# Spreading per-token factors over 64 partitions by DMAs through DRAM in a two-layer encoder kernel

## The chip, the cores and the metric

The kernel runs on one NeuronCore of a Trainium2 chip. The metric is device time in microseconds (us) of one launch. Its program drives five instruction streams that synchronise by semaphores: TensorE (PE, matmuls and transposes, results in PSUM), VectorE (DVE), ScalarE (ACT), GpSimd (POOL) and SyncE (SP), which here does nothing but start DMAs. Each stream runs in order: an instruction that waits holds up everything behind it on its stream.

## The reference

Two layers (`DEPTH` = 2) over 512 tokens of width 1024, all in float32. The part that matters is the first half of a layer, two attention mixers that share one input projection:

```python
proj = einsum('bsd,de->bse', x, w_in)            # q, k, v of both mixers and the gate logits
oa = banded_attention(qa, ka, va, 128, a_sink)   # 8 heads; per token and head: o / denom
for g, (window, dil) in enumerate(((128, 1), (512, 4), (2048, 16))):
    o[g], lse[g] = dilated_attention(qb[g], kb[g], vb[g], window, dil)   # 4 heads each
wts = softmax(stack(lse), axis=0)                # per token and head, over the three groups
ob = einsum('gbsh,gbshd->bshd', wts, stack(o))
h = (ga * (oa @ w_branch_a) + gb * (ob @ w_branch_b)) @ w_out
x = layer_norm(alpha * x + h)                    # then a squared-ReLU MLP and a second layer norm
```

So there are two sorts of factors that belong to one token and one head: `1/denom` of mixer A, and the three group weights (already divided by the softmax sums) of mixer B. Each multiplies the 64 channels of its head's output.

## The kernel before

**Layout.** Activations lie transposed: channels on the 128 partitions, the 512 tokens along the free dimension. Every matrix product is done as three matmuls of float32r halves (`mm3`, lines 279 to 281: high by high, low by high, high by low). A weight set of 128 x 1024 is fetched by SP (`wst`, L248, three buffers), then split by `split` into a rounded high part on ACT (`whi`, L227) and the rest on DVE (`wlo`, L228); `weights(key)` asks for the set two ahead of the one in use.

**Attention.** `unit_a(i)` (four of them) handles two heads of mixer A, `unit_b(sp, g)` (six) two heads of one dilated group. A unit computes scores into the two PSUM banks tagged `s` (`sa`, `sb`, L438), adds the mask and takes the row maximum on DVE (`masked`, L431), takes the exponential on ACT (`exped`, L427, which also sums the rows: the softmax denominators), turns the probabilities by PE transposes into a bank tagged `pt` (`probs_T`, L416) and multiplies them with the values into `f` (128 channels of two heads x 512 tokens). `mix_b(sp)` then makes the weights of the three groups for head pair `sp` (L664 to L699): a tile `e`, in which each partition is a token of one of four blocks and the 24 columns are group, head and block.

**The factors.** In `den` and `e` the tokens lie on partitions; `f` has them along the free dimension. So a factor has to be turned, and repeated over the 64 channels of its head. Before, `widened` (L455) copies the 8 factors of a partition to 512 columns on ACT, and `token_scaled` turns them with four PE transposes into a `pt` bank `rs` (L461) and multiplies `f` by it on DVE (L462). This is done 10 times in a layer: 4 in `unit_a`, 3 in each of the two `mix_b`. In `mix_b` the three scaled groups are then added on POOL (L708) and DVE (L709) and split into `OB[sp]` (`obh`, `obl`).

**What sets the order.** The PE's order in the attention is written out by generators: `fc`, a small forecast of the engines' times, decides when a step of a unit is `able`; in between the projections of the next units and gates (`filler`: `qb`, `kb`, `vb`, `g`, and `ya`, the products of `w_branch_a`) are put. Two units are live at once. The order of the other engines' instructions, SP's DMAs among them, is set by the compiler's scheduler. After the attention, `ya` and gate projections follow, and then `yb`, the first product that reads `OB` (L1099).

Of the kernel before, what the change touches and what calls it, by code (L numbers as in the profile page):

```python
# [10 lines left out]
F32 = mybir.dt.float32  # L11
# [9 lines left out]
P = 128  # L21
S = 512
# [15 lines left out]
HOP = 0.35  # L38
# [162 lines left out]
def build(nc, tc, plan, down, xT, xN, pT, wst, vec, rows, sink, cst, out):  # L201
# [3 lines left out]
    with ctx:  # L205
# [4 lines left out]
        def bank(tag, name):  # L210
            return pp.tile([P, 512], F32, tag=tag, name=name, bufs={"mm": 3, "s": 2, "pt": 2, "o": 1}[tag])


        ident = cp.tile([P, P], F32, name="ident")
# [11 lines left out]
        def split(hi, lo, src):  # L226
            nc.scalar.copy(hi, src)  # L227
            nc.vector.tensor_tensor(lo, src, hi.bitcast(F32), ALU.subtract)  # L228
# [119 lines left out]
        def attention_block(l, av, rp, vt, OA, OB, begun):  # L348
# [81 lines left out]
            def masked(dst, ps, mask, mx):  # L430
                nc.vector.tensor_tensor_reduce(dst, ps, mask, 1.0, NEG, ALU.add, ALU.max, mx)  # L431
                return fc.on("dve", 0.07 + mask.shape[-1] / 960, fc.t + HOP)
# [12 lines left out]
            def join(f, o, r):  # L445
                a, b = slice(r * 64, r * 64 + 64), slice(64 - r * 64, P - r * 64)
                nc.scalar.copy(f[a, :], o[b, :])
                nc.vector.tensor_tensor(f[a, :], o[a, :], f[a, :], ALU.add)
                t = fc.on("dve", 0.6, fc.on("act", 0.48, fc.t + HOP) + HOP) + HOP
                fc.give("o", t)  # L450
                return t

            def widened(c, name, after):
                wide = av.tile([P, 4, 2, 64], F32, tag="wide", name="wide" + name, bufs=1)
                nc.scalar.copy(wide, c.rearrange("p r (j u) -> p j r u", u=1).to_broadcast([P, 4, 2, 64]))  # L455
                return wide, fc.on("act", 0.52, after) + HOP

            def token_scaled(f, wide, name, after):
                R = bank("pt", "rs" + name)
                for j in range(4):  # L460
                    nc.tensor.transpose(R[:, j * P:(j + 1) * P], wide[:, j].rearrange("p r d -> p (r d)"), ident)  # L461
                nc.vector.tensor_tensor(f, f, R, ALU.mult)  # L462
                t = fc.on("dve", 0.6, max(fc.pe(0.43) + HOP, after)) + HOP
                fc.take("pt", t)
                return t


            WIN = [(max(0, P * (j - 1)), min(S, P * (j + 2))) for j in range(4)]
# [2 lines left out]
            def unit_a(i):  # L471
                q, k = held["qa", i], held["ka"]
                nm_ = f"a{l}_{i}"
# [4 lines left out]
                den = av.tile([P, 2, 4], F32, tag="den", name="den" + nm_, bufs=2)  # L478
                ns = nsink.rearrange("p (r i) -> p r i", r=2)[:, :, i]
                ap, ex = {}, {}  # L480
                for j in range(4):
# [6 lines left out]
                    for r in range(2):  # L488
                        ap[r, j] = pr[r][:, POS[j]:POS[j] + w]
                        t = masked(ap[r, j], ss[r][:, :w], cc["ma"][:, mo:mo + w], mx[:, r, j:j + 1])  # L490
                    fc.take("s", t + HOP)
                    nc.vector.scalar_tensor_tensor(nm[:, :, j], mx[:, :, j], -0.125, ns, ALU.mult, ALU.min)
                    t = fc.on("dve", 0.08, t + 0.13) + HOP
# [4 lines left out]
                nc.scalar.activation(se, se, AF.Exp)  # L498
                nc.vector.tensor_tensor(den, den, se, ALU.add)
                nc.vector.reciprocal(den, den)  # L500
                wide, t_wide = widened(den, nm_, ex[1, 3] + 0.6)
                yield lambda: "va" in held
                v, t_v = held["va"]
                f = av.tile([P, S], F32, tag="f", name="f" + nm_, bufs=1)
# [18 lines left out]
                for n, (r, kbs) in enumerate(groups):  # L523
# [7 lines left out]
                    c = 0  # L531
# [6 lines left out]
                    if n % 3 == 2:  # L538
                        t_f = join(f, o, r)
# [3 lines left out]
                held["P"] -= 2  # L543
                if i == 3:
                    held["vv"] -= 1
                yield lambda: fc.open("pt") and fc.t >= t_wide
                t_f = token_scaled(f, wide, nm_, t_f)
                split(OA[i][0], OA[i][1], f)
                forecast_split(S, t_f)

# [113 lines left out]
            def mix_b(sp, cn, cs):  # L664
                nm_ = f"{l}_{sp}"
                fs = [held["og", sp, g] for g in range(3)]
                t = max(x[2] for x in fs)
# [15 lines left out]
                t = fc.on("dve", 0.1, fc.pe(0.17) + HOP) + HOP  # L683
# [3 lines left out]
                e = av.tile([P, 3, 8], F32, tag="e", name="e" + nm_, bufs=1)  # L687
# [12 lines left out]
                t += 2.6  # L700
                for g in range(3):
                    f, t_f, _ = fs[g]
                    wide, t = widened(e[:, g].rearrange("p (s b) -> p s b", s=2), f"{nm_}_{g}", t)
                    yield lambda: fc.t >= t and fc.open("pt")
                    token_scaled(f, wide, f"{nm_}_{g}", t_f)
                    t = fc.t
                f = fs[0][0]
                nc.gpsimd.tensor_tensor(f, f, fs[1][0], ALU.add)  # L708
                nc.vector.tensor_tensor(f, f, fs[2][0], ALU.add)  # L709
# [7 lines left out]
            fc = Forecast()  # L717
# [79 lines left out]
            for i in range(4):  # L797
                waiting["a", i] = (slots(2, "ka", ("qa", i)), lambda i=i: unit_a(i))
# [240 lines left out]
        def pool(name, side="left"):  # L1039
            c = ExitStack()  # L1040
            return c.enter_context(tc.tile_pool(name=name, bufs=1, side=side, reuse_waits="tile")), c.close

        dp = ctx.enter_context(tc.tile_pool(name="dp", bufs=1, space=bass.MemoryType.DRAM))
# [14 lines left out]
        for l in range(DEPTH):  # L1058
# [13 lines left out]
            av, av_close = pool(f"av{l}")  # L1072
# [19 lines left out]
            for u in range(4):  # L1092
                gs = [gate(l, 1, t, vt, rp) for t in (2 * u, 2 * u + 1)]
                w = weights((l, ("bb", u)))
                for n, g in enumerate(gs):
                    t = 2 * u + n
# [268 lines left out]
```

## Time and profile before

| | |
|---|---|
| median of 3 runs | 1545.58 us (1545.32 to 1548.82) |
| profiled execution | 1545.51 us, its span 1543.7 us |
| mean granted TensorE clock | 0.996 |
| VectorE / ScalarE / GpSimd busy | 1089.2 us / 717.4 us / 205.4 us |
| DMA | 162.19 MB, mean 105 GB/s |

The span is what the profiler shows of the execution; 1.8 us lie around it. The attention of the two layers lies from about 28 to 259 us and from 797 to about 1028 us of the span; the rest is the branch and output projections, the gated embedding and the MLP. Which engine limits is read from the busy shares together with the chain of work that ended last: a high busy share of PE says that the PE's own work sets the time, and that a wait counts when the PE stands in it.

### The profile page before, as it was taken

How to read it: one execution, taken by the hardware profiler on the slowest of the kernel's cores; microseconds unless marked ns; L12 is line 12 of the kernel's file. 1: busy time of each engine (PE TensorE's matmuls, PEld its weight loads, DVE VectorE, ACT ScalarE, POOL GpSimd, SP SyncE). 2: the span in 40 equal slices, each digit the busy share in tenths (PEclk: the TensorE clock that was granted, in tenths of full speed). 3: DMA queues.
4: the chain of work that ended last, by engine and by line, in shares of the span. 5: the costliest groups of instructions: out<-in, count | busy, mean ns of one | idle time of the engine just before them, and what ended most of it. 6: DMA issues, size and time to landing. Idle time of an engine off the chain costs nothing.

```text
span 1543.7 us, 19566 instructions
## 1 busy us (share of the span) xinstructions
PE 1516.1 (98%) x7438; PEld 1244.0 (81%) x7438; DVE 1089.2 (71%) x1803; ACT 717.4 (46%) x1192; POOL 205.4 (13%) x161
## 2 busy tenths in 40 slices
PE   9999999999999999999999999999999999999996
PEld 7778788888888888888887778888888888888885
DVE  6778675467568767696877786744575776767868
ACT  4566554344334443434546665542442443444343
POOL 1011110020011120202010101111100211111022
PEclk9999999999999999999999999999999999999998
DMA  6211224244612415142342121254446233241403
GB/s 219 69 55 55 69 69 170 84 131 158 199 65 83 146 45 162 43 149 70 96 149 69 55 68 56 80 164 146 136 136 211 68 99 120 70 135 55 150 1 96
DMA packets 46461, 162.19 MB, mean 105 GB/s; under 512 B 5664, under 2 KB 6048, under 8 KB 46368
## 3 DMA queue, kind: packets, MB, share of 16 engines
q1 hardware_dynamic: 43200, 151.74, 29.3%
q0 software_dynamic: 2448, 8.91, 3.0%
q8 instruction: 58, 0.95, 0.2%
q10 hardware_dynamic: 720, 0.30, 0.1%
q14 instruction: 35, 0.29, 0.1%
HBM read 155.16 MB, written 4.19 MB: 103 GB/s over the span
## 4 chain that ended last, share of the span: by engine, by line
PE 87%; DVE 8%; ACT 2%; issue 1%; DMA 1%; ACTq 0%; SPq 0%; DVEq 0%
PE dn L1017 16%; PE ps_up L280 8%; PE ps_up L279 8%; PE ps_up L281 8%; PE pg L287 2%; PE wo L285 2%; PE wo L287 2%; PE wo L286 2%; PE pg L286 2%; PE pg L285 2%; DVE wlo L228 2%; PE sa L438 1%; PE pta L416 1%; PE ya L279 1%; PE ya L281 1%
## 5 line engine op out<-in xcount | busy, mean ns | idle before, releaser
L228 DVE TENSOR_TENSOR wlo<-wst,whi 128x1024 fp32r<-128x1024 f32 (+1 forms) x172 | 220.7, 1286 | 150.9 <-ACT whi L227 144.3
L227 ACT CAST whi<-wst 128x1024 fp32r<-128x1024 f32 (+1 forms) x172 | 175.7, 1022 | 299.5 <-PE ps_up L280 115.5
L279 PE MATMUL ps_up<-xhi,whi 128*128 128x512 f32 x512 | 199.2, 389 | 0.0
L280 PE MATMUL ps_up<-xlo,whi 128*128 128x512 f32 x512 | 199.2, 389 | 0.0
L281 PE MATMUL ps_up<-xhi,wlo 128*128 128x512 f32 x512 | 199.2, 389 | 0.0
L990 POOL TENSOR_TENSOR hr<-r 128x512 f32<-128x512 f32 x64 | 102.2, 1597 | 551.4 <-ACT r L982 530.9
L279 PEld LDWEIGHTS ps_up<-xhi,whi 128*128 128x128 f32 x512 | 96.1, 188 | 20.0
L281 PEld LDWEIGHTS ps_up<-xhi,wlo 128*128 128x128 f32 x512 | 96.1, 188 | 20.0
L280 PEld LDWEIGHTS ps_up<-xlo,whi 128*128 128x128 f32 x512 | 96.1, 188 | 19.8
L227 ACT CAST whi<-raw 128x1024 fp32r<-128x1024 f32 x56 | 58.0, 1053 | 97.0 <-PE ps_up L280 64.1
L227 ACT CAST dhi<-raw 128x1024 fp32r<-128x1024 f32 x56 | 58.7, 1051 | 82.2 <-PE dn L1017 59.8
L1036 DVE TENSOR_TENSOR y<-y,dn 128x512 f32<-128x512 f32 x96 | 65.2, 681 | 38.5 <-PE dn L1017 38.5
L970 DVE TENSOR_TENSOR raw<-raw,raw 128x1024 f32<-128x1024 f32 x64 | 86.4, 1349 | 0.2
L228 DVE TENSOR_TENSOR wlo<-raw,whi 128x1024 fp32r<-128x1024 f32 x56 | 68.1, 1219 | 14.1 <-ACT whi L227 14.1
L228 DVE TENSOR_TENSOR dlo<-raw,dhi 128x1024 fp32r<-128x1024 f32 x56 | 69.2, 1239 | 5.5 <-ACT dhi L227 5.5
L1017 PE MATMUL dn<-whi,smh 128*128 128x512 f32 x128 | 50.1, 394 | 0.7 <-DVE y L1036 0.7
L1017 PE MATMUL dn<-wlo,smh 128*128 128x512 f32 x128 | 50.6, 395 | 0.2
L287 PE MATMUL pg<-bhi,xlo 128*128 128x512 f32 x128 | 49.9, 390 | 0.6 <-DVE xlo L914 0.6
L1017 PE MATMUL dn<-whi,sml 128*128 128x512 f32 x128 | 49.9, 390 | 0.0
L285 PE MATMUL pg<-bhi,xhi 128*128 128x512 f32 x128 | 49.9, 390 | 0.0
L1017 PE MATMUL dn<-dhi,smh 128*128 128x512 f32 x128 | 49.9, 390 | 0.0
L1017 PE MATMUL dn<-dlo,smh 128*128 128x512 f32 x128 | 49.8, 389 | 0.0
(846 smaller groups left out, 3889.0 us busy)
## 6 DMA issues: line engine op xcount, KB each, us to landing
wst<-wst SPq DMA_DIRECT2D x187, 512.0 KB, 3.5
raw<-wst SPq DMA_DIRECT2D x64, 512.0 KB, 4.2
y<-rows POOLq DMA_DIRECT2D x14, 512.0 KB, 7.6
row<-rows SPq DMA_DIRECT2D x7, 512.0 KB, 9.8
wst<-wst SPq DMA_DIRECT2D x9, 256.0 KB, 2.7
xs<-xT SPq DMA_DIRECT2D x8, 256.0 KB, 5.7
y<-xN SPq DMA_DIRECT2D x4, 512.0 KB, 6.9
kept<-y SPq DMA_DIRECT2D x4, 512.0 KB, 2.9
```

Source lines behind the costliest of these rows:

```text
L227: nc.scalar.copy(hi, src)
L228: nc.vector.tensor_tensor(lo, src, hi.bitcast(F32), ALU.subtract)
L279: nc.tensor.matmul(ps, w[0][:, s], x[0], start=start, stop=False, skip_group_check=part)
L280: nc.tensor.matmul(ps, w[0][:, s], x[1], start=False, stop=False, skip_group_check=part)
L281: nc.tensor.matmul(ps, w[1][:, s], x[0], start=False, stop=stop, skip_group_check=part)
L285: nc.tensor.matmul(ps, x[0], w[0][:, c], start=start, stop=False)
L286: nc.tensor.matmul(ps, x[0], w[1][:, c], start=False, stop=False)
L287: nc.tensor.matmul(ps, x[1], w[0][:, c], start=False, stop=stop)
L970: nc.vector.tensor_tensor(to, to, other, ALU.add)
L990: nc.gpsimd.tensor_tensor(h.rearrange("p s t -> p (s t)"), r, r, ALU.mult)
L1017: nc.tensor.matmul(ps[s], a[:, k, tok], w[b][:, cols], start=first and not (k or m), stop=k == 3 and m == 2, skip_group_check=True)
L1036: return nc.vector.tensor_tensor(to, to, ps, ALU.subtract if n in (2, 4, 5) else ALU.add)
```

## The change

`widened` and `token_scaled` lose the copy and the transposes. A new function `spread_out` writes the 8 factors of each of 128 partitions into a DRAM tile `line` of 2 x 512 (head by token; each of the 1024 values is 4 bytes with no neighbour from the same partition), and then reads each head's row of 512 back onto 64 partitions of the tile `wide`. All three DMAs are started by SP. `line` has six buffers, `wide` one. The multiplication takes `wide` from SBUF instead of `rs` from PSUM. `dp` is the pool of DRAM tiles, which was there before.

```diff
-            def widened(c, name, after):
-                wide = av.tile([P, 4, 2, 64], F32, tag="wide", name="wide" + name, bufs=1)
-                nc.scalar.copy(wide, c.rearrange("p r (j u) -> p j r u", u=1).to_broadcast([P, 4, 2, 64]))
-                return wide, fc.on("act", 0.52, after) + HOP
-
-            def token_scaled(f, wide, name, after):
-                R = bank("pt", "rs" + name)
-                for j in range(4):
-                    nc.tensor.transpose(R[:, j * P:(j + 1) * P], wide[:, j].rearrange("p r d -> p (r d)"), ident)
+            def spread_out(c, name, after):
+
+                line = dp.tile([2, S], F32, tag="line", name="line" + name, bufs=6)
+                nc.sync.dma_start(line.rearrange("r (j p) -> p r j", j=4), c)
+                R = av.tile([P, S], F32, tag="wide", name="wide" + name, bufs=1)
+                for r in range(2):
+                    nc.sync.dma_start(R[r * 64:r * 64 + 64, :], line[r].partition_broadcast(64))
+                return R, after + 5.0
+
+            def token_scaled(f, R, after):
                 nc.vector.tensor_tensor(f, f, R, ALU.mult)
-                t = fc.on("dve", 0.6, max(fc.pe(0.43) + HOP, after)) + HOP
-                fc.take("pt", t)
-                return t
+                return fc.on("dve", 0.6, after) + HOP
...
-                wide, t_wide = widened(den, nm_, ex[1, 3] + 0.6)
+                R, t_R = spread_out(den, nm_, ex[1, 3] + 0.6)
...
-                yield lambda: fc.open("pt") and fc.t >= t_wide
-                t_f = token_scaled(f, wide, nm_, t_f)
+                t_f = token_scaled(f, R, max(t_f, t_R))
...
-                    wide, t = widened(e[:, g].rearrange("p (s b) -> p s b", s=2), f"{nm_}_{g}", t)
-                    yield lambda: fc.t >= t and fc.open("pt")
-                    token_scaled(f, wide, f"{nm_}_{g}", t_f)
-                    t = fc.t
+                    R, t_R = spread_out(e[:, g].rearrange("p (s b) -> p s b", s=2), f"{nm_}_{g}", t)
+                    token_scaled(f, R, max(t_f, t_R))
```

In the changed kernel the DMA to DRAM is L456, the DMAs that read it back are L459, and the multiplication is L463. Three places of the new order follow; layer 1 has the same order as layer 0.

SP, layer 0, at the weights of the first head pair (`mix_b(0)`); the names are the factors' tiles (`line_0_g`, `wide_0_g` of group g) and the weight sets `wst`. Before, only weight fetches stand here.

```order
L456 DMA line_0_0_1875<-e_0_1860 128x8x1 [waits DMAHW5_49,DVE_49,Activation_49]
L456 DMA line_0_1_1881<-e_0_1860 128x8x1 [waits DVE_49]
L456 DMA line_0_2_1887<-e_0_1860 128x8x1 [waits DVE_49]
L459 DMA wide_0_0_1877<-line_0_0_1875 64x512 [waits DMAHW5_49]
L459 DMA wide_0_0_1877<-line_0_0_1875 64x512
L248 DMA wst_2125<-wst 128x1024 [waits DMAHW2_49,DVE_49]
L459 DMA wide_0_1_1883<-line_0_1_1881 64x512 [waits DMAHW3_49,DMAHW1_49,DMAHW6_49,DMAHW0_49,DVE_49]
L459 DMA wide_0_1_1883<-line_0_1_1881 64x512 [waits DMAHW4_49]
L248 DMA wst_2187<-wst 128x1024 [waits DVE_49]
L459 DMA wide_0_2_1889<-line_0_2_1887 64x512 [waits DMAHW4_49,DMAHW7_49,DMAHW3_49,DVE_49]
```

All three `line` DMAs are started first, then the two halves of `wide_0_0`, which wait until its `line` has landed. `wide_0_1` waits on DVE, since the single buffer is free only after the multiplication of group 0, and `wide_0_2` after that of group 1.

DVE, layer 0, the same place, before the change (`ql_kb`: low part of the keys of the next unit; `pb` with `sb`: masking of that unit's scores; `cn`: its row maxima; `ogb`: the groups' outputs, multiplied in place):

```order
L462 TENSOR_TENSOR ogb_0_0_1362<-ogb_0_0_1362,rs_0_0_1935 128x512 [waits PE_49]
L228 TENSOR_TENSOR ql_kb_0_1913<-t_kb_0_1907,qh_kb_0_1912 128x512 [waits Activation_49]
L462 TENSOR_TENSOR ogb_0_1_1509<-ogb_0_1_1509,rs_0_1_1949 128x512 [waits PE_49]
L228 TENSOR_TENSOR wlo_2010<-wst_2007,whi_2009 128x1024 [waits DMAHW7_49,PE_49,Activation_49]
L431 ISA pb_1_0_0_1964,mxb_1_0_1963<-sb_1_0_0_0_1970,ct_157 128x192 [waits PE_49]
...
L462 TENSOR_TENSOR ogb_0_2_1751<-ogb_0_2_1751,rs_0_2_1993 128x512 [waits PE_49]
L584 TENSOR_SCALAR cn_1_328<-mxb_1_0_1963 128x2x2 [waits DVE_49]
```

And now, where the multiplications wait for DMAs:

```order
L228 TENSOR_TENSOR ql_kb_0_1925<-t_kb_0_1919,qh_kb_0_1924 128x512 [waits Activation_49]
L463 TENSOR_TENSOR ogb_0_0_1332<-ogb_0_0_1332,wide_0_0_1877 128x512 [waits DMAHW1_49,DMAHW0_49]
L228 TENSOR_TENSOR wlo_1966<-wst_1963,whi_1965 128x1024 [waits DMAHW3_49,PE_49,Activation_49]
L431 ISA pb_1_0_0_1974,mxb_1_0_1973<-sb_1_0_0_0_1980,ct_157 128x192 [waits PE_49]
...
L228 TENSOR_TENSOR vvvb_1_0_2008<-vtvb_1_0_2003,vvvb_1_0_2008 128x8x64 [waits Activation_49]
L463 TENSOR_TENSOR ogb_0_1_1504<-ogb_0_1_1504,wide_0_1_1883 128x512 [waits DMAHW4_49,DMAHW3_49]
L582 TENSOR_SCALAR cn_1_328<-mxb_1_0_1973 128x2x2 [waits DVE_49]
...
L463 TENSOR_TENSOR ogb_0_2_1728<-ogb_0_2_1728,wide_0_2_1889 128x512 [waits DMAHW7_49,DMAHW6_49]
L582 TENSOR_SCALAR cn_1_328<-mxb_1_0_1973 128x2x2 [waits DVE_49]
L373 STREAM_SHUFFLE sw_qb_1_2056<-ps_('qb', 1, 1)_1969 128x512 [waits PE_49]
```

The multiplication of group 0 now stands ahead of the masking of the next unit's first scores, the one of group 1 ahead of its first row maxima (the first `cn`), and the one of group 2 ahead of the second `cn`, on which the unit's remaining exponentials wait.

DVE, layer 0, at the second head pair (`mix_b(1)`), now (`gate` with `ya`: the first branch's products, taken out of PSUM; `wlo`: weight sets that PE needs one after the other):

```order
L463 TENSOR_TENSOR ogb_1_0_2049<-ogb_1_0_2049,wide_1_0_2607 128x512 [waits DMAHW4_49,DMAHW3_49]
L781 SCALAR_TENSOR_TENSOR gate_0_3_1756<-gate_0_3_1756,ya_1_1_2686 128x512 [waits PE_49]
L228 TENSOR_TENSOR wlo_2703<-wst_2700,whi_2702 128x1024 [waits DMAHW6_49,Activation_49]
L463 TENSOR_TENSOR ogb_1_1_2262<-ogb_1_1_2262,wide_1_1_2613 128x512 [waits DMAHW7_49,DMAHW6_49]
L463 TENSOR_TENSOR ogb_1_2_2478<-ogb_1_2_2478,wide_1_2_2619 128x512 [waits DMAHW2_49,DMAHW1_49]
L228 TENSOR_TENSOR wlo_2736<-wst_2733,whi_2735 128x1024 [waits PE_49,Activation_49]
L705 TENSOR_TENSOR ogb_1_0_2049<-ogb_1_0_2049,ogb_1_2_2478 128x512 [waits DVE_49,Pool_49]
```

The multiplications of groups 1 and 2 stand directly behind each other, though the second needs a reload of `wide` that starts after the first. The weight set `wlo_2736` stands behind both.

## The prediction

> **What bounds the kernel now.** I read first the page's busy shares, then its chain of work that ended last.
>
> ```profile
> PE 1516.1 (98%) x7438; PEld 1244.0 (81%) x7438; DVE 1089.2 (71%) x1803; ACT 717.4 (46%) x1192; POOL 205.4 (13%) x161
> PE 87%; DVE 8%; ACT 2%; issue 1%; DMA 1%; ACTq 0%; SPq 0%; DVEq 0%
> ```
>
> PE is never far from busy, and 87% of the chain is its own work. So PE time that goes is gained, unless a new wait brings PE to a stand; work that leaves ACT (46% busy) gains nothing by itself. The second share of the chain is DVE, and it lies largely in the attention, where the changed lines are. What matters is therefore how long PE stands when DVE or SP wait for the new DMAs.
>
> **What is removed.** The tile view of `rs` and `wide` counts it (durations are min/median/max in ns):
>
> ```profile
> L461 PE MATMUL rs<-ident,wide x48: 270/272/329, 180.1 to 1024.0; 128*128 128x128 f32 x48
> L461 PE MATMUL rsa<-ident,widea x32: 270/272/273, 70.7 to 905.5; 128*128 128x128 f32 x32
> L455 ACT COPY wide<-e x12: 616/618/620, 179.4 to 1022.7; 128x512 f32<-128x512 f32 x12
> L455 ACT COPY widea<-dena x8: 607/618/620, 57.2 to 886.4; 128x512 f32<-128x512 f32 x8
> L462 DVE TENSOR_TENSOR fa<-fa,rsa x8: 679/684/690, 75.4 to 909.3; 128x512 f32<-128x512 f32 x8
> ```
>
> 80 transposes are 20 groups of four. Durations of matmuls overlap, so a group's price is read from starts, in the timeline of PE (start, length, in us):
>
> ```profile
> 252.48 0.39 PE L281 MATMUL ya<-oah,wlo 128*128 128x512 f32 x1
> 252.71 0.60 PE L461 MATMUL rs<-ident,wide 128*128 128x128 f32 x4
> 253.06 0.48 PE L279 MATMUL ya<-oah,whi 128*128 128x512 f32 x1
> 253.38 0.39 PE L280 MATMUL ya<-oal,whi 128*128 128x512 f32 x1
> ...
> 253.61 0.40 PE L281 MATMUL ya<-oah,wlo 128*128 128x512 f32 x1
> ```
>
> A matmul of 512 columns starts 0.23 us after the one before (253.38 to 253.61). From 252.48 to 253.38 passed 0.90 where two such steps would take 0.46: the group costs **0.44 us**. The first group of each `mix_b` costs more, since PE also waits for the copy on ACT:
>
> ```profile
> 179.42 0.39 PE L281 MATMUL ps_('vb', 1, 0)_1922<-xhi,wlo 128*128 128x512 f32 x1
> ...
> 180.10 0.65 PE L461 MATMUL rs<-ident,wide 128*128 128x128 f32 x4 [0.29 <-ACT wide L455]
> ...
> 180.82 0.40 PE L280 MATMUL ps_('vb', 1, 0)_1922<-xlo,whi 128*128 128x512 f32 x1
> ...
> 249.99 0.39 PE L281 MATMUL ya<-oah,wlo 128*128 128x512 f32 x1
> ...
> 251.55 0.39 PE L280 MATMUL ya<-oal,whi 128*128 128x512 f32 x1
> ```
>
> 1.40 - 0.46 = 0.94 and 1.56 - 0.46 = 1.10. A layer has eight plain groups and these two: 8 x 0.44 + 0.94 + 1.10 = 5.56; two layers **11.1 us**, all in PE's stream. The ACT copies (20 x 0.62 = 12.4 us) count nothing beyond the waits just included. The multiplication stays; its second operand comes from SBUF, which I cost at nothing.
>
> **What is added: the DMAs' length.** No row shows a DMA that stores 4-byte pieces. The nearest is the load of the sinks: 128 rows of 32 bytes, 8 packets on each of 16 engines. Below are its landing time, that of 256 KB (what the two halves of `wide` write), the spread of the sinks' landing, and two answers about packets: the first for 781 to 786 us (the sinks alone on that queue), the second for 1538 to 1543.7 (a store of 128 rows of 2 KB).
>
> ```profile
> sk<-sink ACTq DMA_DIRECT2D x2, 4.0 KB, 4.0
> wst<-wst SPq DMA_DIRECT2D x9, 256.0 KB, 2.7
> ...
> DMA to landing us min/median/max: 3.6/4.0/4.4
> ...
> q10 hardware_dynamic: 144, 0.00, 1.8%
> ...
> q10 hardware_dynamic: 144, 0.26, 12.6%
> ```
>
> 1.8% of 16 engines x 5 us is 1.44 us for 144 packets, **10 ns** each; 12.6% of 16 x 5.7 is 11.5 us, **80 ns** each. A line has 64 packets on each engine. A 4-byte store should lie between: it is as small as the first or smaller, but written to DRAM like the second. I take the middle in ratio, **28 ns**, and keep both ends. One `line` then lands 4.0 + 56 x 0.028 = 5.6 us after its issue.
>
> [...]
>
> **In the four `unit_a` of a layer this is hidden.** The ACT copy of the first stands at 57.2 us and the multiplication at 75.4: 18 us between, against 5.6 + 0.4 + 2.7 = 8.7 for the new chain. In the others the reload may start once the previous multiplication is through, again some 18 us ahead. SP, held meanwhile, fetches weights later; the waits of SP show how much room there is (total, times, longest):
>
> ```profile
> SPq L248 <- DVE wlo L228: 877.9, 155, 26.0
> ```
>
> SP mostly waits for a free buffer, 5.7 us on average, and the set it then fetches is used two sets later. I cost this at nothing; if the cover were gone, what SP was held would show in PE.
>
> **In `mix_b(0)` it is not hidden.** The weights `e` are ready at the end of the first row, about 179.4, when ACT took them up:
>
> ```profile
> 178.37 1.12 DVE L699 TENSOR_TENSOR e<-e,mn 128x8 f32<-128x8 f32 x3
> ...
> 176.93 0.39 PE L279 MATMUL ps_('vb', 1, 0)_1922<-xhi,whi 128*128 128x512 f32 x1
> 183.89 0.36 PE L438 MATMUL sb<-qh_kb,qh_qb 64*128 64x192 f32 x2
> ...
> 184.77 0.66 PE L461 MATMUL rs<-ident,wide 128*128 128x128 f32 x4
> 184.85 1.23 DVE L228 TENSOR_TENSOR wlo<-wst,whi 128x1024 fp32r<-128x1024 f32 x1 [1.54 <-PE sb L438]
> 185.99 0.35 DVE L431 CUSTOM_DVE_ANT_0 pb<-sb,ct 128x192 f32<-128x192 f32 x1
> ...
> 187.23 0.68 DVE L462 TENSOR_TENSOR ogb<-ogb,rs 128x512 f32<-128x512 f32 x1
> ...
> 190.59 0.17 DVE L584 TENSOR_SCALAR cn<-mxb 128x4 f32<-128x4 f32 x1
> ...
> 190.79 0.51 ACT L427 ACTIVATE pb<-pb,cn 128x256 f32<-128x256 f32 x1 [0.22 <-DVE cn L584]
> ```
>
> `line_0_0` lands at 179.4 + 5.6 = 185.0. The reload alone would land 0.4 (the issue of its first half, as long as one of the four of `y` further down) + 2.7 later, 188.1; but the two other lines are queued ahead of it, 2 x 64 x 0.028 = 3.6 us, so with its own 8 packets an engine (0.6) it lands at **189.2**. DVE reaches the multiplication near 183 and stands there. Behind it: the multiplication (0.68), a `wlo` (1.23), the masks (185.99 to 187.23, 1.24): the two score banks are free at about 192.4. In the new order PE would want them at 187.9: from 176.93, 24 + 3 matmuls (6.2), twelve score matmuls (183.89 to 184.77, 0.9), four transposes (0.44), 15 matmuls (3.4). **First wait: 4.5 us.**
>
> Then group 1: DVE gets there at 193.0 (masks, then `vvvb`, as long as a multiplication), when its reload (189.9 + 3.1) is just in. Group 2's reload can start at 193.7 and is in at 196.8; DVE stands again, multiplies, makes `cn`, and ACT gives the exponential at 198.3. PE, going on at 192.4 with 0.9 + 3.4 + 0.3 us of work, wants it at 197.0. **Second wait: 1.3 us.** Together 5.8 a layer, 11.6 in two: the waits eat the gain (-11.1 + 11.6 = +0.5).
>
> **The clock** is a further term. The end of the trace shows what a gap does: the last matmul, and the windows after it (PEclk is the third figure from the right).
>
> ```profile
> 1530.02 0.39 PE L1017 MATMUL dn<-dhi,axl 128*128 128x512 f32 x1
> ...
> 1531.00:1533.00 2.00, 0.00 (x0) 0.00 (x0) 1.86 (x7) 0.47 (x1) 1.51 (x3) 0.88 1.01 195
> 1533.00:1536.00 3.00, 0.00 (x0) 0.00 (x0) 2.49 (x7) 1.24 (x2) 1.65 (x2) 0.50 1.05 203
> ```
>
> A mean of 0.88 means 1.00 until 1532.5 and 0.50 from there: it fell 2.1 us after the last matmul. A first wait of 4.5 us is longer. What follows at half rate is not shown: bounds are 0, and the 4.6 us of work up to the second wait taking 4.6 longer, of which 1.3 would have been waited for, 3.3 a layer. I take the middle, 1.7 a layer, **3.4** in all.
>
> [...]
>
> **In `mix_b(1)` DVE stands but PE does not.** Same chain from 250.2 (249.9 plus 0.3 for `e`): multiplications at 260.0, 263.8, 267.6, and the weight sets `wlo_2703` and `wlo_2736` behind them at 262.6 and 269.5.
>
> ```profile
> 249.90 0.32 DVE L699 TENSOR_TENSOR e<-e,mn 128x8 f32<-128x8 f32 x3
> 255.74 1.90 SPq L1080 DMA_DIRECT2D y<-xN  x4
> ...
> 269.97 0.39 PE L279 MATMUL ya<-oah,whi 128*128 128x512 f32 x1
> ...
> 275.41 0.39 PE L279 MATMUL ya<-oah,whi 128*128 128x512 f32 x1
> ...
> 291.73 0.39 PE L279 MATMUL yb<-obh,whi 128*128 128x512 f32 x1
> ```
>
> PE uses these two sets at 269.97 and 275.41, and `OB` (ready near 272) at 291.73. Cover of 6 us and more; the loads of `y` behind it on SP (now at 255.74) are needed later still.
>
> **The sum.** 1545.5 (profiled execution, as good as the median 1545.58) - 11.1 + 11.6 + 3.4 = **1549.4 us**, slower by 0.25%: no change that can be told, since about 0.3% (4.6 us) is what a measurement of this kernel can tell.
>
> **The rivals.**
> Slower, the small stores: each ns a packet moves the landing by 56 + 128 packets, 0.18 us a layer. From 30 ns the loss is over 0.3%; at 45 ns the time is 1555.7, at 80 ns 1568, and `wlo_2703` would then be late too (to 1576). For it: 4 bytes without a neighbour; against: the 10 ns of the nearest row. 0.30.
> Slower, the clock: half rate all through the 4.6 us gives 1552.6, and more if it lasts past the second wait. For it: the fall at 2.1 us. 0.12.
> Faster: packets at 10 ns put `wide_0_0` at 187.1, the waits are 2.4 + 1.3, the clock has hardly time to fall: 1541.8; with a `line` landing in 3.6 (the sinks' quicker load) and a shorter `wide`, under 1540.9. All hidden would be 1534.4. Against it: even then DVE stands until 186. 0.15.
>
> **How the numbers follow.** Forecast (1541 to 1550) 0.43, slower by the stores 0.30, by the clock 0.12, faster 0.15. So faster 0.15, same 0.43, slower 0.42. The range 1540 to 1566 leaves out about 0.1 at each end: packets near 80 ns above, nearly hidden chains below. The forecast's own range is 1541 to 1550.
>
> **What would show it.** PE with 80 matmuls fewer; new waits of DVE L463 for DMA, long ones at the first and third of `mix_b(0)` and at all of `mix_b(1)`; PE waiting at `sb` (L438) for DVE, then at `ptb` (L416) for ACT, near 188 and 197; a clock below 1.00 there; `line` landing 5.6 us after issue. Wrong: `line` in 4 us or under, or over 8; PE waits in `unit_a`; weight sets waiting for SP.

## The result and the profile after

| | before | after |
|---|---|---|
| time, us (median, lowest to highest) | 1546.07 (1545.32 to 1548.82, 4 runs) | 1607.43 (1605.02 to 1609.11, 4 runs) |
| ratio, 95% interval | | 1.0397 (1.0384 to 1.041) |
| profiled execution: time, span | 1545.51, 1543.7 | 1606.72, 1604.9 |
| mean granted clock | 0.996 | 0.977 |

The change costs 61 us, 4%. The forecast was 1549.4 us and the range ended at 1566: the prediction was wrong, on the side of the rival "the small stores".

The page of the changed kernel, its busy shares, chain of work by engine and by line, and the group of the three multiplications of `mix_b` (busy and mean ns, then the idle time of VectorE ahead of them and what ended it):

```profile
PE 1523.5 (95%) x7358; PEld 1247.4 (78%) x7358; DVE 1092.4 (68%) x1803; ACT 705.9 (44%) x1172; POOL 201.0 (13%) x161
...
PE 77%; DVE 9%; DMA 9%; issue 2%; ACT 2%; SPq 0%; DVEq 0%; ACTq 0%
...
L463 DVE TENSOR_TENSOR ogb<-ogb,wide 128x512 f32<-128x512 f32 x12 | 8.3, 692 | 88.4 <-DMA wide<-line 88.4
```

The 80 transposes are gone from the instruction count (7438 to 7358). DMA has risen from 1% of the chain to 9%, and VectorE stands 88.4 us at 12 multiplications, 7.4 us each in the mean; most of it lies at the first of each `mix_b` (19.81 us in the rows below). The 8 multiplications of `unit_a`, on the same line, wait for no transfer. What TensorE waits for, in order of the total (us in total, times, longest):

```profile
PE sb L438 <- DVE mxb L431: 33.0, 2, 16.8
PE ya L279 <- ACT gate L842: 9.3, 2, 5.6
PE ya L279 <- DVE gate L781: 8.0, 2, 4.3
PE oa L442 <- DVE fa L448: 4.3, 4, 1.7
PE ob L442 <- DVE fa L448: 3.9, 2, 2.0
```

The first row is `mix_b(0)`, once a layer; the second and third are `mix_b(1)`; the last two are `unit_a`. Why the wait of `mix_b(0)` is so long stands in the timeline of its first layer: the queue of SP, the multiplications, and TensorE on both sides of its stop.

```profile
180.79 2.21 SPq L456 DMA_DIRECT2D line<-e  x3
191.83 1.09 SPq L459 DMA_DIRECT2D wide<-line  x2
...
204.52 1.08 SPq L459 DMA_DIRECT2D wide<-line  x2
...
203.81 0.69 DVE L463 TENSOR_TENSOR ogb<-ogb,wide 128x512 f32<-128x512 f32 x1 [19.81 <-DMA wide<-line]
208.41 0.69 DVE L463 TENSOR_TENSOR ogb<-ogb,wide 128x512 f32<-128x512 f32 x1 [0.93 <-DMA wide<-line]
212.60 0.69 DVE L463 TENSOR_TENSOR ogb<-ogb,wide 128x512 f32<-128x512 f32 x1 [2.19 <-DMA wide<-line]
...
189.13 0.39 PE L281 MATMUL ps_('qb', 1, 1)_1969<-xhi,wlo 128*128 128x512 f32 x1
206.31 1.20 PE L438 MATMUL sb<-qh_kb,qh_qb 64*128 64x256 f32 x2 [16.79 <-DVE mxb L431]
```

SP may issue the reload only when the first `line` has landed: 191.83 - 180.79 = 11.0 us. Then `wide` is 12 us on the way (191.83 to 203.81). The prediction gave the way from `e` to the landing of `wide` 9.8 us (179.4 to 189.2); from the first store to the multiplication it took 23. Two more stores stand between. The second and the third `line`, each in the DMA view of its own issue (how many, KB each, us from issue to landing):

```profile
line<-e SPq DMA_DIRECT2D x1, 4.0 KB, 14.7
line<-e SPq DMA_DIRECT2D x1, 4.0 KB, 17.5
```

They were issued at 181.22 and 182.43, so the three land at 191.8, 195.9 and 199.9, and the two halves of `wide` follow at 203.4 and 203.7. The windows of the same place (columns: PE, PEld, DVE, ACT, POOL busy, then granted clock, busy share of the DMA engines, GB/s) show two more things:

```profile
185.00:190.00 5.00, 4.52 (x27) 3.41 (x25) 0.00 (x0) 1.02 (x3) 0.00 (x0) 1.00 0.06 0
190.00:195.00 5.00, 0.00 (x0) 0.00 (x0) 0.00 (x0) 0.00 (x0) 0.00 (x0) 0.80 0.00 0
195.00:200.00 5.00, 0.00 (x0) 0.00 (x0) 0.00 (x0) 0.00 (x0) 0.00 (x0) 0.50 0.07 13
...
205.00:210.00 5.00, 3.65 (x16) 2.89 (x17) 4.07 (x17) 0.73 (x3) 0.76 (x1) 0.50 0.48 157
210.00:215.00 5.00, 5.00 (x20) 4.01 (x19) 2.81 (x10) 3.77 (x14) 1.35 (x2) 0.65 0.17 52
```

While everything waits for these stores, the DMA engines' busy share is 0.06, 0.00 and 0.07, and they move 0, 0 and 13 GB/s: it is not the amount of data that takes the time. And the clock, once halved, stays so after TensorE goes on at 206.31: a mean of 0.65 over the window 210 to 215, of values that are 0.50 and 1.00 in the windows around it, means 0.50 until 213.5, so 7.2 us of work ran at half rate.

The DMA issues of the changed kernel (how many, KB each, median us from issue to landing):

```profile
wide<-line SPq DMA_DIRECT2D x24, 128.0 KB, 3.1
...
widea<-linea SPq DMA_DIRECT2D x16, 128.0 KB, 4.7
...
line<-e SPq DMA_DIRECT2D x12, 4.0 KB, 11.9
linea<-dena SPq DMA_DIRECT2D x8, 4.0 KB, 10.2
```

### The profile page after: what moved, and what is told of

It reads as the page before. It is cut to its first block, busy times and chain, and to the rows that moved or that the text cites. A ratio compares the mean times of both kernels' runs of the same rounds, so it can differ in the third digit from the quotient of the medians.

```text
span 1604.9 us, 19490 instructions
## 1 busy us (share of the span) xinstructions
PE 1523.5 (95%) x7358; PEld 1247.4 (78%) x7358; DVE 1092.4 (68%) x1803; ACT 705.9 (44%) x1172; POOL 201.0 (13%) x161
## 4 chain that ended last, share of the span: by engine, by line
PE 77%; DVE 9%; DMA 9%; issue 2%; ACT 2%; SPq 0%; DVEq 0%; ACTq 0%
PE dn L1013 16%; PE ps_up L279 7%; PE ps_up L281 7%; PE ps_up L280 7%; DMA wide<-line 4%; DMA line<-e 3%; PE pg L287 2%; PE wo L285 2%; PE wo L287 2%; PE wo L286 2%; PE pg L286 2%; PE pg L285 2%; DVE wlo L228 2%; DMA wst<-wst 2%; PE sa L438 1%
## 5 line engine op out<-in xcount | busy, mean ns | idle before, releaser
L228 DVE TENSOR_TENSOR wlo<-raw,whi 128x1024 fp32r<-128x1024 f32 x56 | 68.1, 1219 | 14.1 <-ACT whi L227 14.1
L463 DVE TENSOR_TENSOR ogb<-ogb,wide 128x512 f32<-128x512 f32 x12 | 8.3, 692 | 88.4 <-DMA wide<-line 88.4
```

## The experiments

Each is told against the kernel before, run beside it.

**One part alone (e1, e2).** The edits put the old `widened` and the transposes back in one of the two callers; e1:

```diff
-                    R, t_R = spread_out(e[:, g].rearrange("p (s b) -> p s b", s=2), f"{nm_}_{g}", t)
-                    token_scaled(f, R, max(t_f, t_R))
+                    wide, t = widened(e[:, g].rearrange("p (s b) -> p s b", s=2), f"{nm_}_{g}", t)
+                    yield lambda: fc.t >= t and fc.open("pt")
+                    pe_scaled(f, wide, f"{nm_}_{g}", t_f)
+                    t = fc.t
```

> Only the softmax denominators of unit_a go through DRAM; mix_b transposes as in the kernel before. Theory 1 (the loss is made in mix_b, where the engines wait for `wide`; in unit_a the round trip of some 14 us lies beside the attention): 32 transposes in 8 groups of 0.44 us are gone and nothing is added on the path, 1546.1 - 3.5 = 1542.5 us, range 1540 to 1546. Theory 2 (the sync queue is held: of its 152 us of waits for these transfers 72 are unit_a's, and behind them stand the weight loads): 72/152 of the 61 us lost are made here, 1546 + 29 = 1575 us, and in no case under 1550. In the profile theory 1 wants no PE wait over 1 us that ends in a transfer or in a multiplication of unit_a.

> Only the weights of mix_b go through DRAM; unit_a transposes as in the kernel before. Theory 1 (mix_b makes the whole loss): the changed kernel's time and the 3.5 us that unit_a had saved, 1607.4 + 3.5 = 1611 us, range 1605 to 1615. Theory 2 (held sync queue, shared with unit_a): 1546 + 32 = 1578 us, range 1565 to 1590. Together with the kernel that changes unit_a alone the two differences to the kernel before should sum to +61 us if the parts are independent.

e1 took 1550.33 us (before 1546.38; ratio 1.0024, 1.0014 to 1.0035), e2 1607.33 (ratio 1.0391, 1.0377 to 1.0405). So `mix_b` makes the loss, and the held SP queue does not; but `unit_a` did not gain 3.5 us, it lost 4. The waits of TensorE in e1 between 100 and 160 us, and behind them the windows where the first of these lies (columns as above):

```profile
PE ob L442 <- DVE fa L448: 2.0, 1, 2.0
PE oa L442 <- DVE fa L448: 1.7, 1, 1.7
```
```profile
135.00:140.00 5.00, 3.04 (x35) 2.81 (x35) 4.91 (x7) 2.13 (x4) 1.04 (x1) 0.96 0.32 101
140.00:145.00 5.00, 5.00 (x21) 4.33 (x20) 5.00 (x23) 3.60 (x10) 0.00 (x0) 0.70 0.02 7
```

Neither wait ends in a transfer: VectorE reaches `fa` late, TensorE stops for 2.0 us, and the clock falls to a mean of 0.70 behind it. That is a matter of which instruction stands where.

**The same with the old order (e5).** The change takes two bookings out of the kernel's forecast of TensorE along with the transposes, so the forecast places later units elsewhere. e5 leaves the bookings in:

```diff
-                t_f = token_scaled(f, R, max(t_f, t_R))
+                yield lambda: fc.open("pt") and fc.t >= t_R
+                nc.vector.tensor_tensor(f, f, R, ALU.mult)
+                t_f = fc.on("dve", 0.6, max(fc.pe(0.43) + HOP, t_f)) + HOP
+                fc.take("pt", t_f)
```

> The kernel of e1 (unit_a alone through DRAM), with the forecast left as it was before the change: the wait of unit_a's last step and the time it books on TensorE stay, so that TensorE's order is that of the kernel before without its 32 transposes. e1 took 1550.3 us, 7.5 us more than the 3.5 us of removed transposes allow. Theory 1 (the 7.5 us come from the new order alone: a wait of 2.0 us for `fa` near 136 us, and the lower clock behind it): 1546.4 - 3.5 = 1542.9 us, range 1541 to 1545.5. Theory 2 (they come from the transfers: held sync queue, small packets in the way of the weights): 1549 to 1552 us, as in e1.

1544.18 us (before 1546.27; ratio 0.9986, 0.9978 to 0.9995). With TensorE's order that of before less 32 transposes, the 6 us that e1 lies above it are gone, and the transfers of `unit_a` are hidden: 2.1 of the 3.5 us arrive. e5 is the one kernel of the study whose interval lies below the kernel before; the gain is 0.14%, less than the 0.3% set as the bound.

**Where the wait stands (e4, e6).** In e4 the program places each multiplication of `mix_b(0)` at least 16 us of forecast behind its store; in e6 it is also tied on VectorE behind a mask of a later unit:

```diff
+                    t += LATE if g == 0 else 6.0
+                    yield lambda: fc.t >= t
+                    with tc.issue_after(held["mask"].ins):
+                        token_scaled(fs[g][0], R, t)
```

> unit_a through DRAM; mix_b(0) through DRAM, but each multiplication stands in the program at least 16 us (by the kernel's own forecast) behind its store, so that VectorE does the next unit's work in between, and each store is issued only when the multiplication ahead of it is placed; mix_b(1) transposes as before. Theory 1 (the loss is VectorE standing at the multiplication, in order, with the next unit's masks behind it): the stall of mix_b(0) is gone, the removed groups are 8 of unit_a and 6 of mix_b(0), 14 x 0.44 + 2 x 0.5 for the two first ones = 7.2 us, 1546.1 - 7.2 = 1539 us, range 1536 to 1548. Theory 2 (the small packets or the held sync queue cost time wherever they lie): over 1555 us, since 14 of the 20 round trips are still there.

e4: 1577.12 us (before 1546.38; ratio 1.0198, 1.0184 to 1.0212): inside the bound of theory 2 (over 1555), but e4 did not set up what theory 1 was about, so it decides nothing between them. The scheduler had moved the multiplication forward again to where it stood, right behind the last work that was ready, and VectorE waited at it as before:

```profile
183.87 0.69 DVE L228 TENSOR_TENSOR ql_kb<-t_kb,qh_kb 128x512 fp32r<-128x512 f32 x1 [0.69 <-ACT qh_kb L227]
202.25 0.69 DVE L463 TENSOR_TENSOR ogb<-ogb,wide 128x512 f32<-128x512 f32 x1 [17.69 <-DMA wide<-line]
```

> As e5, and mix_b(0) through DRAM too, with TensorE's order kept; the three multiplications are tied on VectorE behind the masks of later units (row 353 of its order; in e4 the scheduler had put the first at about row 300, as in the changed kernel), some 30 us and more behind the store of e; mix_b(1) transposes. Theory 1 (what costs is VectorE standing in order at a multiplication whose `wide` comes 20 us behind e): no wait for `wide` is left, 14 of the 20 groups of transposes are saved, 14 x 0.44 + 2 x 0.5 = 7.2 us, 1546.4 - 7.2 = 1539.2 us, range 1537 to 1544. Theory 2 (the stores and loads cost time wherever they lie): over 1548 us.

e6: 1544.98 us (before 1546.27; ratio 0.9992, 0.9983 to 1.0001). With the multiplications out of the way, the stores and loads of `mix_b(0)` cost nothing that can be measured, though the stores are as slow as before (a median of 10.8 us). They are also spread here, two at 178 and the third at 188.6 in layer 0, so e6 alone does not tell the later place from the wider spacing; either way theory 2 falls. Theory 1 holds in its mechanism and misses its range (to 1544) by 1 us: of its 7.2 us only 1.3 arrive. TensorE has 5.8 us less work than before (1516.1 to 1510.3) but waits more, most of all here, where it waited 1.6 us before:

```profile
PE ob L444 <- DVE ptlb L229: 3.3, 2, 1.7
```

**What holds the second transfer up (e3).** The three stores of `mix_b` go through ScalarE's queue, the loads stay in SP's: `nc.scalar.dma_start` in place of `nc.sync.dma_start` for `line`.

> The changed kernel with the three stores of mix_b issued by ScalarE on its own queue; their loads stay on the sync queue. Theory 1a (the first `wide` of a mix_b waits 8.6 us because it stands in the queue behind the second and third store): `wide` lands some 3 us behind its issue in place of 11.5, the first multiplication comes 8.6 us earlier, and 4 mix_b by 8.6 us are the most that comes back: 1607.4 - 34 = 1573 us; with half of it hidden elsewhere 1590; range 1570 to 1592. Theory 1b (the 1024 small packets of each store hold the DMA engines, whichever queue they came by): the load still waits for the packets of the other stores, no more than 5 us come back, 1602 to 1608 us.

1603.93 us (before 1546.38; ratio 1.0372, 1.0356 to 1.0388): some 3.5 us come back, theory 1b. The rows of its first `mix_b(0)`, on SP and VectorE:

```profile
190.18 1.09 SPq L459 DMA_DIRECT2D wide<-line  x2
...
201.84 0.69 DVE L463 TENSOR_TENSOR ogb<-ogb,wide 128x512 f32<-128x512 f32 x1 [15.53 <-DMA wide<-line]
```

No store stands ahead of `wide` in its own queue any more, and still it is 11.7 us on the way. Two unfinished stores stand in ScalarE's queue meanwhile (they land at 199.8 and 201.4); without such stores (e8, below) the same load takes 3.5 us. One weight fetch does stand ahead of `wide`, and it is held up itself: SP issued it at 182.08, 1.2 us behind the first store on the other queue. It reads another place of DRAM, and the median of its kind in this run is 3.6 us; the DMA view from 182.0 to 182.3 has

```profile
wst<-wst SPq DMA_DIRECT2D x1, 512.0 KB, 14.1
```

So what the stores hold up is not only the reading of what they write. In what way they do it no row shows.

**Is it the number of pieces? (e7, e8).** e7 stores only the first row of each `line` and loads it for both heads, so it leaves out the second head's factors; e8 stores rows in place of columns:

```diff
-                nc.sync.dma_start(line.rearrange("r (j p) -> p r j", j=4), c)
+                nc.sync.dma_start(line[0].rearrange("(j p) -> p j", j=4), c[:, 0, :])
```
```diff
+                nc.tensor.transpose(t3[:24, :P], e.rearrange("p g v -> p (g v)"), ident)
+                nc.vector.tensor_copy(rows8, t3[:24, :P])
...
+                nc.sync.dma_start(line.rearrange("r (j p) -> (r j) p", j=4), c)
```

> The changed kernel, but each `line` stores only the first of its two rows, 512 pieces of 4 bytes in place of 1024, and both halves of `wide` are loaded from that row; the second row's factors are left out. Theory 1 (packets: 64 packets on each engine at some 66 ns, 4.2 us a store, and the first `wide` waits for all three stores): 32 packets fewer in each of three stores, 6.3 us off the first multiplication of each mix_b, 4 x 6.3 = 25 us at most, 1582 us, range 1575 to 1595; a line lands 2.1 us sooner. Theory 2 (the price is the write to DRAM and the read behind it, whatever the number of pieces): landing times and the time stay, 1600 to 1609 us.

> The changed kernel, but in mix_b one transpose turns the 24 columns of e into 24 rows of 128, VectorE copies them, and each `line` is stored from them in 8 pieces of 512 bytes in place of 1024 of 4; unit_a as in the changed kernel. Theory 1 (the number of small packets sets the landing): `line` lands in about 4 us, `wide` 3 us later with nothing ahead of it, the first multiplication stands some 10 us behind e in place of 23; 4 mix_b by up to 13 us come back, less some 1 us each for transpose and copy: 1607 - 48 = 1559 us at best, range 1555 to 1580. Theory 2 (the round trip itself): `line` still lands in 8 us or more and no more than 12 us come back, over 1595 us.

e7: 1609.07 us (before 1546.27; ratio 1.0412, 1.0396 to 1.0427): half the pieces change nothing in the time, and a `line` of `mix_b` lands after 12.6 us in the median (11.9 with all). So the price is not one per piece, the form in which the prediction had it. e8: 1557.66 us (ratio 1.0075, 1.0061 to 1.0089): 50 of the 61 us come back. Its `mix_b(0)`, in the rows of SP and VectorE:

```profile
182.53 1.03 SPq L456 DMA_DIRECT2D line<-rows  x3
186.03 1.09 SPq L459 DMA_DIRECT2D wide<-line  x2
...
189.48 0.69 DVE L463 TENSOR_TENSOR ogb<-ogb,wide 128x512 f32<-128x512 f32 x1 [1.50 <-DMA wide<-line]
```

The same 4 KB land within 3.5 us, and `wide` follows in 3.5. The trip through DRAM is not dear; this way of writing is. Of the 11 us that are left, 4 may be those of e1, which changes `unit_a` alone; the rest was not taken apart.

**The store by itself (e11, e12).** In the kernel before, each `unit_a` gets one more store of `den` to DRAM that nothing reads. The kernel's time stays (1545.53 and 1545.97 us, one run each). Two of the eight stores:

```diff
+                    nc.sync.dma_start(scratch("adj", 2, S).rearrange("r (j p) -> p r j", j=4), c)
+                    nc.sync.dma_start(scratch("apart", 2, S, 16)[:, :, 0].rearrange("r (j p) -> p (r j)", j=4), c.rearrange("p r j -> p (r j)"))
```

> The kernel before, with one store more in each unit_a, from the same den of 128x8 to DRAM, that nothing reads: unit 0 the store of the changed kernel (1024 pieces of 4 bytes, neighbours in DRAM come from neighbouring partitions), unit 1 its first row alone (512 pieces), unit 2 the same 1024 pieces each in a 64-byte block of its own, unit 3 128 pieces of 32 bytes. The reading is the time from issue to landing. Theory 1 (price per piece): 10, 7, 10 and 4 us. Theory 2 (pieces from different partitions that fall into one block wait for each other): 10, 10 (e7 took no less), 5 and 4 us. Theory 3 (a fixed price of a small write): 10, 10, 10 and 4 us or more. The kernel's time stays within 4 us of before.

> As e11, with other stores: unit 0 1024 pieces of 4 bytes, the 8 of a partition in one 64-byte block of their own (every second word), unit 1 a single column, 128 pieces of 4 bytes side by side, unit 2 1024 pieces of 4 bytes, each 512 bytes from the next, unit 3 256 pieces of 4 bytes in two runs of 128. Theory 1 (price per piece): 10, 4, 10 and 5 us. Theory 2 (pieces from different partitions in one block wait for each other): 5, 9, 5 and 9 us. Theory 3 (a fixed price of a small write): 10 in all four.

The DMA issues of e11 (number, KB, median us to landing; the two of each agree within 0.9 us):

```profile
adja<-dena SPq DMA_DIRECT2D x2, 4.0 KB, 11.2
halfa<-dena SPq DMA_DIRECT2D x2, 2.0 KB, 9.0
aparta<-dena SPq DMA_DIRECT2D x2, 4.0 KB, 2.7
wholea<-dena SPq DMA_DIRECT2D x2, 4.0 KB, 1.8
```

and of e12:

```profile
mixeda<-dena SPq DMA_DIRECT2D x2, 4.0 KB, 6.1
cola<-dena SPq DMA_DIRECT2D x2, 0.5 KB, 7.6
fara<-dena SPq DMA_DIRECT2D x2, 4.0 KB, 2.6
twoa<-dena SPq DMA_DIRECT2D x2, 1.0 KB, 8.6
```

1024 pieces of 4 bytes land in 2.7 us when each has 64 bytes to itself, and in 11.2 when they are neighbours; 128 neighbours (`col`) take 7.6. Theory 2 tells the dear from the cheap, theories 1 and 3 fall. But the cheap ones are cheaper than it had them (2.7, 2.6 and 1.8 for 5, 5 and 4), and eight pieces of one partition in 64 bytes of their own are dear too (`mixed`, 6.1): what the dear ones have in common is several 4-byte pieces within 64 bytes, whether from one partition or from many. The number of pieces counts for less: 128, 256, 512 and 1024 neighbours take 7.6, 8.6, 9.0 and 11.2 us. An estimate from these rows, if what `col` and `mixed` take above the 2.6 us of `far` is shared out among the pieces within 64 bytes: (7.6 - 2.6) / 16 = 0.31 us for each of 16, (6.1 - 2.6) / 8 = 0.44 for each of eight. That such pieces are written one after the other is not shown, and the 1024 neighbours, also 16 in 64 bytes, give more: (11.2 - 2.6) / 16 = 0.54. The 64 bytes are the spacing that was tried; between the 8 bytes of `mixed` and these 64 nothing was. Two 32-byte pieces in 64 bytes (`whole`) are not dear. What does this no row shows. Each kind of store stood in one of the four units alone, but the unit is not what tells them apart: in the changed kernel, which stores neighbours in every unit, no `linea` whose landing is in the trace took less than 8.5 us, and the reload of the fourth unit of layer 0 was issued 9.6 us behind its store.

**The two `mix_b` apart, and all of it, with the old order (e9, e10, e14).** On e5's base, as in e5 with the bookings kept, `mix_b(0)` alone, `mix_b(1)` alone, then both:

> As e5 (unit_a through DRAM, TensorE's order kept), and mix_b(0) through DRAM with the multiplications where the kernel before had them; mix_b(1) transposes. Theory 1 (the stop in mix_b(0) is the larger part of the loss): per layer a stop of 16.8 us and some 3.5 us lost to the halved clock behind it, less 1.8 us of transposes, 18.5 us; 1544.2 + 37 = 1581 us, range 1574 to 1590. Theory 2 (mix_b(1), with nothing but ya behind it, makes the larger part): under 1568 us.

> As e9, but mix_b(1) through DRAM and mix_b(0) by transposes. Theory 1 (VectorE stands at the multiplication with the next gate and weight behind it, and TensorE with 6 us of work in hand stops twice): per layer stops of 4.3 and 5.6 us, some 4 us at half clock, less 1.8 us of transposes, 12 us; 1544.2 + 24 = 1568 us, range 1558 to 1576. Theory 2, as the prediction had it (TensorE has work in hand and does not stop): 1541 to 1547 us. With e9 the parts should sum to the loss of the changed kernel: 1.2 per cent of it is order (e1 against e5, 6 us), the rest these two.

> The whole change with TensorE's order kept: unit_a as in e5, both mix_b as in e9 and e10. Theory 1 (the parts add up): 1544.2 + 38.4 + 24.9 = 1607.5 us, range 1603 to 1611, the changed kernel's own time, so that its new order costs nothing on the whole. Theory 2 (the new order costs the changed kernel the 6 us by which e1 lies over e5): 1599 to 1602 us.

e9: 1582.56 us (before 1545.86; ratio 1.0235, 1.022 to 1.0251). e10: 1569.06 (ratio 1.0153, 1.0136 to 1.017). e14: 1611.51 (before 1546.63; ratio 1.0419, 1.0404 to 1.0435). Against before these are +36.7, +23.2 and +64.9, and e5 is -2.1: the parts would sum to 36.7 + 23.2 + 2.1 = 62.0, 3 us under e14. Theory 1 of e14 is missed by half a microsecond at its upper end (1611), theory 2 by 9: the new order, which costs 6 us in e1, costs the changed kernel nothing on the whole (1607.43 against 1611.51).

In e9 the stops are 36.2 us, 18.1 a layer. The row of the waits:

```profile
PE sb L438 <- DVE mxb L431: 36.2, 2, 18.4
```

TensorE goes on at 202.79, and the windows (columns as above) give the clock:

```profile
200.00:205.00 5.00, 2.17 (x13) 1.71 (x13) 3.24 (x11) 0.00 (x0) 0.00 (x0) 0.50 0.45 156
205.00:210.00 5.00, 5.00 (x16) 3.97 (x16) 3.50 (x14) 3.94 (x16) 1.28 (x1) 0.63 0.26 98
```

0.63 puts the return at 208.7: 5.9 us at half rate, 2.95 lost if TensorE would have been busy throughout. 18.1 + 2.95 - 1.82 for the groups removed (0.94 + 2 x 0.44) is 19.2 a layer; measured against e5 are (36.7 + 2.1) / 2 = 19.4. That the two agree supports the clock's share, but no run took it away.

In e10 TensorE stops twice a layer; the first two rows are its stops, and the others the VectorE rows ahead of the first:

```profile
270.92 0.76 PE L279 MATMUL ya<-oah,whi 128*128 128x512 f32 x1 [4.05 <-DVE gate L809]
282.85 0.79 PE L279 MATMUL ya<-oah,whi 128*128 128x512 f32 x1 [3.74 <-ACT gate L870]
...
269.48 0.69 DVE L723 TENSOR_TENSOR ogb<-ogb,wide 128x512 f32<-128x512 f32 x1 [15.48 <-DMA wide<-line]
270.09 0.68 DVE L809 SCALAR_TENSOR_TENSOR gate<-gate,ya 128x512 f32<-128x512 f32 x1
```

Behind the waiting multiplication stands not only the weight set that the prediction counted, but a `gate` that reads a PSUM bank of `ya` and so frees it; the order that is shown ahead of the prediction has this `gate` in the same place. The second stop is ScalarE's: its `obh` waits 17.77 us for the sum of the three, and the `gate` behind it frees a bank too.

**The clock (e13).** e9 with 70 matmuls, whose results nothing reads, in the stop:

```diff
+                        if sp and jj:
+                            fill = bank("o", "fill" + nm_)
+                            for _ in range(70):
+                                nc.tensor.matmul(fill, k[0][:, :P], q[0], start=True, stop=True)
```

> As e9, with 70 matmuls of 128x512 more in each layer, whose results nothing reads, on TensorE right ahead of the score matmuls that stand 18 us for VectorE; at 0.23 us they take 16.1 us of that stop. Theory 1 (besides the stop itself e9 pays for the halved clock behind it: 38.4 us against e5, less 36.2 us of stops, plus 3.6 us of transposes saved, leaves 5.8 us): the clock stays up, 1582.6 - 5.8 = 1576.8 us, range 1574.5 to 1579.5. Theory 2 (the 5.8 us are other waits, or the work at half clock lies beside VectorE's backlog and costs nothing): 1582 us or more.

1593.06 us (before 1546.63; ratio 1.0302, 1.0285 to 1.0319): 10 us slower than e9. That lies inside the bound of theory 2 (1582 or more), but not for its reason, and the run decides neither. Two things spoiled it. The 3.0 us that it left idle were enough to halve the clock. The extra matmuls and the scores behind them, in the timeline:

```profile
183.69 16.16 PE L588 MATMUL fillb<-qh_qb,qh_kb 128*128 128x512 f32 x70
202.85 1.20 PE L438 MATMUL sb<-qh_kb,qh_qb 64*128 64x256 f32 x2 [3.00 <-DVE mxb L431]
```

The windows behind it:

```profile
200.00:205.00 5.00, 2.10 (x12) 1.64 (x13) 3.34 (x11) 0.00 (x0) 0.00 (x0) 0.76 0.46 166
205.00:210.00 5.00, 5.00 (x14) 3.94 (x14) 2.02 (x5) 1.97 (x8) 1.28 (x1) 0.56 0.30 93
210.00:215.00 5.00, 2.10 (x13) 1.52 (x12) 2.56 (x11) 2.30 (x8) 0.00 (x0) 1.00 0.00 0
```

and VectorE's order changed around the extra work, the third multiplication now ahead of the next unit's second masks, with new waits behind it (TensorE is busy 2.10 us of the last window). The clock's price stands on the windows of e9, not on this run.

## Why the prediction was wrong

- **The gain** (80 transposes, 5.56 us a layer): right as far as it goes; e5 and e6 show that what leaves TensorE's stream arrives only in part (2.1 of 3.5 us, 1.3 of 7.2).
- **`unit_a` hidden**: right for the transfers (e5), though they took 10.2 + 4.7 us where 8.7 was reckoned; the cover was 18. What the step left out is that a forecast without the transposes orders TensorE anew (e1, 6 us).
- **The price of a store** is the step that failed. It took 28 ns a packet between ends of 10 and 80, and had a `line` land 5.6 us after its issue; 11.0 were measured here, 10.2 in the median of `unit_a`. Its form was wrong. Half the packets (e7) cost the same, and as many packets set apart cost 2.7 us (e11). Neither row that it was bounded by, a load of 32-byte rows and a store of 2 KB rows, writes many small pieces side by side.
- **The two other lines ahead of `wide`**: the mechanism was named and mis-sized. 3.6 us were reckoned; the third `line` landed 8.1 us behind the first, and `wide` took 12.0 against a median of 3.1, some 9 more. It is not the place in the queue (e3).
- **The waits of TensorE in `mix_b(0)`**: the place and the chain were right (`sb` for VectorE, at 189), 4.5 + 1.3 us were forecast, 16.8 came. The second wait, for the exponentials, is not among the waits.
- **The clock**: 1.7 us a layer were put in, and 3.3 as the end. 7.2 us at half rate cost 3.6 if TensorE would have been busy throughout; e9 gives 2.95. By the means of the windows, between values of 0.50 and 1.00, the clock stood at half from 193.0 (0.80 over 190 to 195) to 213.5 in the changed kernel, from 188.2 (0.82 over 185 to 190) to 208.7 in e9 and from 202.6 to 209.4 in e13, which is 20.5, 20.5 and 6.8 us. The work done at half rate was 7.2 us in the changed kernel and 5.9 in e9; what sets when the clock returns no run shows.
- **`mix_b(1)`** was put at nothing, on 6 us of cover for two weight sets and a late use of `OB`: it costs 12.6 us a layer by e10, (23.2 + 2.1) / 2. The cover was read for what TensorE reads, not for where it writes. What TensorE waited for was a PSUM bank, freed by a `gate` behind the multiplication on VectorE and by one behind `obh` on ScalarE.
- **The rival "small stores"** had the right cause and a chance of 0.30, but its price at its far end (1568, or 1576) was linear in packets and had of `mix_b(1)` a late weight set alone, so the range ended 41 us short.

## What to carry to other kernels

A store that scatters a column of a tile into a compact row of DRAM is to be measured before it is priced: here 4-byte pieces side by side took 4 times as long as the same pieces 64 bytes apart (11.2 us against 2.7, e11), and turning the column into rows first, in `mix_b`, brought back 50 of the 61 us (e8). When an in-order engine gets a wait (19.81 us of VectorE here, and 16.79 of TensorE behind it), list all that stands behind it, the instructions that free a PSUM bank above all, and not only those that make an operand. And the transfers of `mix_b(0)` were hidden where their consumer stood late in the order in which its engine is issued (e6, 1544.98 us); a later place in the program did not do that, since the scheduler moved the consumer forward again (e4, 1577.12 us).

## What the runs showed that was not expected

- Several 4-byte pieces within 64 bytes: 11.2 us for 1024 neighbouring pieces, 7.6 for 128, 2.7 for 1024 apart; from 185 to 200 us, while such stores of the changed kernel were open, the DMA engines showed a busy share of 0.00 to 0.07. 4-byte pieces 512 bytes apart landed in 2.6 us, so the size of a piece alone is not what costs here.
- Such stores hold back loads of another queue (e3: a weight fetch took 14.1 us where 3.6 is the median, and `wide` 11.7 us from issue to use).
- After a stop of 17 to 18 us the clock stayed at half for 5.9 to 7.2 us of work, and a stop of 3.0 us was enough to halve it (e13); in e1 it was at half for some 3.4 us behind a stop of 2.0 us (0.4 us by the mean of 0.96 over 135 to 140, and 3.0 by that of 0.70 over 140 to 145).
